# Two matmuls of 256 columns become one of 512 in the mixer, and the state-space scan runs in two blocks of 128 steps

## The chip, the cores and the metric

The kernel runs on one core of one Trainium2 chip. The metric is the device time of one execution in microseconds, the lower the better. A core has a matrix engine (TensorE, PE in the profile; its weight loads are shown apart as PEld), a vector engine (VectorE, DVE), an activation engine (ScalarE, ACT), a general engine (GpSimd, POOL) and a queue that starts transfers (SyncE, SP). The engines run side by side. Each works through its own list of instructions in order, and an instruction at the head of a list that has to wait holds up all behind it.

## What is computed

One layer over 256 tokens of width 2048, all in float32. A mixer with two parallel branches comes first, then a mixture-of-experts FFN.

```
h = rms_norm(x);  proj = h @ w_in                    # 2048 -> 512 + 1536 + 1536 + 2*2048
u_s5, x_lru, y_lru = proj[:512], proj[512:2048], proj[2048:3584]
g_s5, g_lru = sigmoid(proj[3584:] + b_gate)          # two gates of 2048
out_s5  = s5_branch(u_s5)                            # complex diagonal state space, 32 groups x 64 states
out_lru = rglru_branch(x_lru, y_lru)                 # conv of 4, two gates, real linear recurrence, * gelu(y_lru)
x = x + (g_s5 * (out_s5 @ w_proj_s5) + g_lru * (out_lru @ w_proj_lru)) @ w_out
x = x + moe(rms_norm(x));  return rms_norm(x)
# s5_branch: states_t = lam_bar * states_(t-1) + b_bar u_t;  y = real(c states) + d u;  gelu, then a GLU
```

## The kernel before

Tokens lie along the free dimension (256 columns, `T`), features along the 128 partitions, so an activation matrix of 2048 features is 16 tiles (`KD`) of 128 x 256. Matmuls use a rounded float32 type. To keep full precision each operand is held as a high part and a low part, and one product is three matmuls into the same bank (`mm3`, L103 to L106): high weight by high input, high weight by low input, low weight by high input. Each has 256 columns and its own weight load. Here a "triple" means these three. `split` (L93) makes the two parts of a weight: ACT copies 1024 (or 768) columns to the rounded type (L99), DVE subtracts (L100); four buffers hold halves of units ahead of PE. Every weight unit of 1 MB is loaded on SP's queue (`load_unit`, L140).

The mixer runs in these stages:

- The first four units give `u` (L174), and about 30 us on the tables of the state-space branch are made on DVE: powers of a rotation, `loc_*` for steps 0 to 16 inside a block and `blk_*` for 16 blocks (`powers`, L360; `d_loc` and `d_blk`, L386).
- Twelve heads of the recurrent branch follow in four groups of three (L570). A head takes three `in_unit`s (L398) of 16 triples each: its y part (into `part` through Gelu, L579), its x part (`lru_head`, L520, with the conv reading the bank directly) and one gate unit (`gate_lru`, L565; ACT reads the bank). After the first and second group stands `s5_chunk(0)` and `s5_chunk(1)` (L409), after the fourth `s5_chunk(2)`; four more gate units; then `s5_chunk(3)`.
- The projection of the recurrent branch (L602): 16 units of 12 triples, each taken out of its bank by one DVE instruction (L611).
- 16 more gate units into `gs5` (L613), the GLU (L624, 16 triples of `mm3` with the state-space output), and the projection of the state-space branch (L651): 16 outputs of four triples, each taken out of its bank by DVE (L662), added on POOL (L663), and cut into high and low parts by ACT and DVE (L648, L649).
- `w_out` (L726), where the moving operand is 512 columns of weight, and the experts, whose 201 MB are streamed.

`s5_chunk(c)` handles four slices of 128 states. For each slice PE projects `u` into a bank of PSUM (`mid`, L422); six DVE instructions of 256 elements rotate it (L430 to L435). Per pair of slices come two scans (real and imaginary, L444), a scan over the 16 block ends with 18 small instructions around it (L453 to L477), the two scans again, and six instructions of 512 to rotate back (L483 to L488). PE then multiplies by `c` (L493) and DVE adds the skip term (L495).

There are four `acc` banks, two `mid` and two `aux` banks of PSUM. The order of each engine's list isn't written by hand. A planner puts the instructions out in time order, ready ones first by priority, which is the order of the program, except where `tc.high_priority(AHEAD)` moves a block ahead (the splits, the loads, what empties an `in_unit`'s bank). Lines L611 and L662 and all of `s5_chunk` have no such mark. A tile with a `tag` takes one of `bufs` buffers; where none is free, the first write waits until the last reader of an earlier tile of that tag has run.

Of the kernel before, what the change touches and what calls it, by code (L numbers as in the profile page):

```python
# [9 lines left out]
F32 = mybir.dt.float32  # L10
# [8 lines left out]
P = 128  # L19
# [16 lines left out]
def block_kernel(  # L36
# [70 lines left out]

    def mm3w(ps, ahi, alo, whi, wlo, first, last):
        PE.matmul(ps, ahi, whi, start=first, stop=False)
        PE.matmul(ps, alo, whi, start=False, stop=False)  # L110
        PE.matmul(ps, ahi, wlo, start=False, stop=last)
# [22 lines left out]
    hT = [hp.tile([P, KD, T], F32R, name=f"hT_{w}") for w in ("hi", "lo")]  # L134
    hT_hi, hT_lo = ([t[:, k, :] for k in range(KD)] for t in hT)
# [169 lines left out]
    blk_c = tb_.tile([P, 16, LOC], F32, name="blk_c")  # L305
    blk_s = tb_.tile([P, 16, LOC], F32, name="blk_s")
# [53 lines left out]
    def powers(tc_, ts_):  # L360
# [3 lines left out]
        while n < 16:  # L364
# [13 lines left out]
    powers(loc_c, loc_s)  # L378
    V.tensor_copy(blk_c[:, :, 1], loc_c[:, :, 16])
    V.tensor_copy(blk_s[:, :, 1], loc_s[:, :, 16])  # L380
    powers(blk_c, blk_s)
    rho16 = t16("rho16")
    V.tensor_tensor(rho16, rho, rho, op=ALU.mult)
    for _ in range(3):
        V.tensor_tensor(rho16, rho16, rho16, op=ALU.mult)
    d_loc = tb_.tile([P, 16, 16], F32, name="d_loc")  # L386
    d_blk = tb_.tile([P, 16, 16], F32, name="d_blk")
    V.tensor_copy(d_loc, rho[:, :, None].to_broadcast([P, 16, 16]))
    V.tensor_copy(d_blk, rho16[:, :, None].to_broadcast([P, 16, 16]))
    V.memset(d_loc[:, :, 0], 0.0)  # L390
    V.memset(d_blk[:, :, 0], 0.0)
# [6 lines left out]
    def in_unit(u, a_hi=hT_hi, a_lo=hT_lo, bank=acc_bank):  # L398
        raw = load_unit(w_in[u], 2048)
        ps = bank()[:, :T]  # L400
        for hf in range(2):
            hi, lo = split(raw[:, hf * 1024:(hf + 1) * 1024], 1024)
            for kk in range(8):
                k = hf * 8 + kk
                cs_ = slice(kk * P, (kk + 1) * P)
                mm3(ps, hi[:, cs_], lo[:, cs_], a_hi[k], a_lo[k], k == 0, k == KD - 1)
        return ps

    def s5_chunk(c):  # L409
        yps[c] = aux_bank()  # L410
        SB = 2
        for sb in range(4 // SB):
            bz = mp.tile([P, 2, SB, T], F32, tag="bz", bufs=2, name=nm("bz"))
            gz = mp.tile([P, 2, SB, T], F32, tag="gz", bufs=2, name=nm("gz"))
            s0 = 4 * c + sb * SB
            for i in range(SB):
                s = s0 + i
                q = s % 4
                rows = slice(32 * q, 32 * q + 32)
                ps = mid_bank()  # L420
                for ri in range(2):
                    PE.matmul(ps[:, ri * T:(ri + 1) * T], bt[rows, c, ri, :], uT[rows, c, :], start=True, stop=True,  # L422
                              tile_position=(32 * q, 0))
                p3 = ps.rearrange("p (r j t) -> p r j t", r=2, t=16)
                lc = loc_c[:, s, None, 0:16].to_broadcast([P, 16, 16])
                ls = loc_s[:, s, None, 0:16].to_broadcast([P, 16, 16])
                tt = mp.tile([P, 2, T], F32, tag="st", bufs=2, name=nm("st"))
                ttv = tt.rearrange("p r (j t) -> p r j t", t=16)
                bzv = bz[:, :, i, :].rearrange("p r (j t) -> p r j t", t=16)
                V.tensor_tensor(ttv[:, 0], p3[:, 1], ls, op=ALU.mult)  # L430
                V.tensor_tensor(ttv[:, 1], p3[:, 0], ls, op=ALU.mult)
                V.tensor_tensor(bzv[:, 0], p3[:, 0], lc, op=ALU.mult)
                V.tensor_tensor(bzv[:, 1], p3[:, 1], lc, op=ALU.mult)
                V.tensor_tensor(bz[:, 0, i, :], bz[:, 0, i, :], tt[:, 0], op=ALU.add)
                V.tensor_tensor(bz[:, 1, i, :], bz[:, 1, i, :], tt[:, 1], op=ALU.subtract)  # L435
            d3 = mp.tile([P, SB * T], F32, tag="d3", bufs=1, name=nm("d3"))
            A.activation(d3.rearrange("p (s j t) -> p s j t", s=SB, t=16),
                         d_loc[:, s0:s0 + SB, None, :].to_broadcast([P, SB, 16, 16]), AF.Copy)
            bz4 = bz.rearrange("p r s (j t) -> p r s j t", t=16)
            gz4 = gz.rearrange("p r s (j t) -> p r s j t", t=16)  # L440

            def scan():
                for ri in range(2):
                    V.tensor_tensor_scan(gz[:, ri].rearrange("p s t -> p (s t)"), d3,  # L444
                                         bz[:, ri].rearrange("p s t -> p (s t)"), 0.0, op0=ALU.mult, op1=ALU.add)

            scan()

            w = lambda: mp.tile([P, SB, 16], F32, tag="cw", bufs=8, name=nm("cw"))
            bc, bs = blk_c[:, s0:s0 + SB, 0:16], blk_s[:, s0:s0 + SB, 0:16]  # L450
            gr, gi = gz4[:, 0, :, :, 15], gz4[:, 1, :, :, 15]
            t1, t2, yr, yi, vr, vi = w(), w(), w(), w(), w(), w()
            V.tensor_tensor(yr, gr, bc, op=ALU.mult)  # L453
            V.tensor_tensor(t1, gi, bs, op=ALU.mult)
            V.tensor_tensor(yi, gi, bc, op=ALU.mult)
            V.tensor_tensor(t2, gr, bs, op=ALU.mult)
            V.tensor_tensor(yr, yr, t1, op=ALU.add)
            V.tensor_tensor(yi, yi, t2, op=ALU.subtract)
            fl = lambda t: t.rearrange("p s j -> p (s j)")
            db = fl(d_blk[:, s0:s0 + SB, :])  # L460
            V.tensor_tensor_scan(fl(vr), db, fl(yr), 0.0, op0=ALU.mult, op1=ALU.add)
            V.tensor_tensor_scan(fl(vi), db, fl(yi), 0.0, op0=ALU.mult, op1=ALU.add)
            bc, bs = blk_c[:, s0:s0 + SB, 1:16], blk_s[:, s0:s0 + SB, 1:16]
            v_r, v_i = vr[:, :, 0:15], vi[:, :, 0:15]
            t1, t2, yr, yi = w(), w(), w(), w()
            t1, t2, yr, yi = t1[:, :, 0:15], t2[:, :, 0:15], yr[:, :, 0:15], yi[:, :, 0:15]
            V.tensor_tensor(yr, v_r, bc, op=ALU.mult)
            V.tensor_tensor(t1, v_i, bs, op=ALU.mult)
            V.tensor_tensor(yi, v_i, bc, op=ALU.mult)
            V.tensor_tensor(t2, v_r, bs, op=ALU.mult)  # L470
            V.tensor_tensor(yr, yr, t1, op=ALU.subtract)
            V.tensor_tensor(yi, yi, t2, op=ALU.add)
            rb = rho[:, s0:s0 + SB, None].to_broadcast([P, SB, 15])
            V.tensor_tensor(yr, yr, rb, op=ALU.mult)
            V.tensor_tensor(yi, yi, rb, op=ALU.mult)
            V.tensor_tensor(bz4[:, 0, :, 1:16, 0], bz4[:, 0, :, 1:16, 0], yr, op=ALU.add)
            V.tensor_tensor(bz4[:, 1, :, 1:16, 0], bz4[:, 1, :, 1:16, 0], yi, op=ALU.add)  # L477
            scan()
            lc = loc_c[:, s0:s0 + SB, None, 0:16].to_broadcast([P, SB, 16, 16])
            ls = loc_s[:, s0:s0 + SB, None, 0:16].to_broadcast([P, SB, 16, 16])  # L480
            tr = mp.tile([P, SB, T], F32, tag="st", bufs=2, name=nm("so"))
            ti = mp.tile([P, SB, T], F32, tag="st", bufs=2, name=nm("so"))
            V.tensor_tensor(tr.rearrange("p s (j t) -> p s j t", t=16), gz4[:, 1], ls, op=ALU.mult)  # L483
            V.tensor_tensor(ti.rearrange("p s (j t) -> p s j t", t=16), gz4[:, 0], ls, op=ALU.mult)
            V.tensor_tensor(bz4[:, 0], gz4[:, 0], lc, op=ALU.mult)
            V.tensor_tensor(bz4[:, 1], gz4[:, 1], lc, op=ALU.mult)
            V.tensor_tensor(bz[:, 0], bz[:, 0], tr, op=ALU.subtract)
            V.tensor_tensor(bz[:, 1], bz[:, 1], ti, op=ALU.add)  # L488
            for i in range(SB):
                s = s0 + i  # L490
                q = s % 4
                for ri in range(2):
                    PE.matmul(yps[c][32 * q:32 * q + 32, :T], cp[:, s, ri, :], bz[:, ri, i, :],  # L493
                              start=(ri == 0), stop=(ri == 1), tile_position=(0, 32 * q))
        V.scalar_tensor_tensor(uT[:, c, :], uT[:, c, :], col(C_S5D, c), yps[c][:, :T], op0=ALU.mult, op1=ALU.add)  # L495
# [24 lines left out]
    def lru_head(h, ps_in, p_):  # L520
# [7 lines left out]
        with tc.high_priority(AHEAD):  # L528
            A.activation(xc, ps_in, AF.Identity, bias=col(C_CONVB, h), scale=col(C_CONVW, 36 + h))
# [35 lines left out]
    def gate_lru(d):  # L565
        ps = in_unit(44 + d)
        with tc.high_priority(AHEAD):
            A.activation(part[:, d, :], ps, AF.Tanh, bias=hcol(C_BGATE, 16 + d), scale=0.5)
# [557 lines left out]
```

## Time and profile before

| | us |
|---|---|
| median of 3 runs (lowest, highest) | 1090.77 (1089.81, 1092.85) |
| the profiled execution | 1093.92 |
| its span, first to last instruction | 1092.1 |
| PE, DVE, ACT, POOL busy in it | 994.2, 645.6, 379.1, 75.6 |

All times of rows are microseconds from the start of the span, unless marked ns. A matmul's row gives its start and how long it lies in the pipeline (0.28 for 256 columns); the next starts long before that, so PE's pace is read from start to start. The same holds for DVE in a smaller measure: an instruction's row is some 0.08 to 0.09 longer than the distance to the next one's start.

### The profile page before, as it was taken

The page shows a single profiled execution, that of the slowest core. Times are in us where ns is not written, and L with a number is a line of the kernel's source. Part 1 is how long each engine was busy: PE and PEld are TensorE (multiplying, and loading weights), DVE is VectorE, ACT ScalarE, POOL GpSimd, SP SyncE. Part 2 cuts the span into 40 slices and gives each one's busy share as a digit, 9 for nine tenths or more (in the row PEclk, how much of TensorE's full clock was granted, in tenths as well). Part 3 has the DMA queues.
Part 4 walks back from the last instruction along what each step waited for, and adds up shares of the span by engine and source line. Part 5 has one row for each costly group of instructions (what it writes and reads, how often), then busy time and mean ns, then how long its engine had stood idle before and what let it go on. Part 6 is the DMA issues. An engine that isn't in the chain of part 4 may idle for free. (4 is left out here: it accounts for less than half of the span.)

```text
span 1092.1 us, 18171 instructions
## 1 busy us (share of the span) xinstructions
PE 994.2 (91%) x7435; PEld 749.4 (69%) x7435; DVE 645.6 (59%) x1356; ACT 379.1 (35%) x591; POOL 75.6 (7%) x76
## 2 busy tenths in 40 slices
PE   5999999999999999999999999999988979797872
PEld 5999899998989999998889945445443424343220
DVE  7899999999999964458544433333333312232225
ACT  5568547577633354445434110111110101011102
POOL 4001201223200000006000000000000000000000
PEclk9999999999999999999999999989998989999897
DMA  7655444454244555554979699999999999999991
GB/s 274 212 171 201 155 158 151 157 178 165 97 147 158 184 190 191 193 182 166 392 290 373 247 393 419 375 419 420 419 419 420 419 420 418 420 420 419 420 383 80
DMA packets 45164, 308.93 MB, mean 283 GB/s; under 512 B 5040, under 2 KB 6736, under 8 KB 9744
## 3 DMA queue, kind: packets, MB, share of 16 engines
q1 hardware_dynamic: 44784, 306.84, 72.5%
q8 instruction: 60, 0.98, 0.4%
q0 software_dynamic: 288, 0.85, 0.4%
q14 instruction: 32, 0.26, 0.1%
HBM read 305.57 MB, written 2.10 MB: 282 GB/s over the span
## 5 line engine op out<-in xcount | busy, mean ns | idle before, releaser
L100 DVE TENSOR_TENSOR wlo<-raw,whi 128x1024 fp32r<-128x1024 f32 (+1 forms) x194 | 230.2, 1189 | 98.0 <-ACT whi L99 97.6
L99 ACT ACTIVATE whi<-raw 128x1024 fp32r<-128x1024 f32 (+1 forms) x194 | 197.5, 1022 | 226.8 <-PE acc L105 163.5
L106 PE MATMUL acc<-hT_hi,wlo 128*128 128x256 f32 x848 | 238.8, 282 | 0.0
L105 PE MATMUL acc<-hT_lo,whi 128*128 128x256 f32 x848 | 238.8, 282 | 0.0
L104 PE MATMUL acc<-hT_hi,whi 128*128 128x256 f32 x848 | 238.2, 282 | 0.0
L990 DVE TENSOR_TENSOR once<-acc,once 128x512 f32<-128x512 f32 x128 | 79.8, 685 | 141.0 <-PE acc L986 141.0
L105 PEld LDWEIGHTS acc<-hT_lo,whi 128*128 128x128 f32 x848 | 159.6, 188 | 2.6 <-issue 2.6
L106 PEld LDWEIGHTS acc<-hT_hi,wlo 128*128 128x128 f32 x848 | 159.5, 188 | 2.1 <-issue 2.1
L104 PEld LDWEIGHTS acc<-hT_hi,whi 128*128 128x128 f32 x848 | 159.2, 188 | 2.4 <-issue 2.4
L104 PE MATMUL acc<-br,whi 128*128 128x256 f32 x336 | 95.9, 291 | 8.1 <-ACT br L177 7.7
L105 PE MATMUL acc<-br,whi 128*128 128x256 f32 x336 | 96.8, 290 | 2.4 <-DVE br L178 2.2
L106 PE MATMUL acc<-br,wlo 128*128 128x256 f32 x336 | 96.0, 290 | 2.2 <-DVE wlo L100 2.2
L986 PE MATMUL acc<-ysb,sct 32*128 32x512 f32 x512 | 95.9, 682 | 1.5 <-DVE once L990 0.8
L942 PE MATMUL mid<-eraw,once 128*32 128x512 f32 x512 | 66.0, 632 | 23.8 <-DMA eraw<-in_w_exp_dram 23.8
L918 PEld LDWEIGHTS aux<-sel,x 128*128 128x128 f32 x512 | 61.0, 195 | 31.0 <-issue 20.8
L974 PE MATMUL mid<-eraw,act 128*32 128x512 f32 x504 | 67.8, 658 | 10.2 <-DVE act L955 8.2
L942 PE MATMUL mid<-eraw,xTe 128*32 128x512 f32 x488 | 61.1, 616 | 16.5 <-DMA eraw<-in_w_exp_dram 16.5
L104 PEld LDWEIGHTS acc<-br,whi 128*128 128x128 f32 x336 | 65.7, 198 | 10.0 <-ACT br L177 7.7
L945 ACT ACTIVATE gus<-mid 128x512 f32<-128x512 f32 x32 | 19.1, 597 | 153.6 <-PE mid L942 153.6
L918 PE MATMUL aux<-sel,x 128*128 128x128 f32 x512 | 67.5, 285 | 5.3 <-DVE sct L967 5.3
L105 PEld LDWEIGHTS acc<-br,whi 128*128 128x128 f32 x336 | 66.1, 197 | 4.4 <-DVE br L178 2.7
L106 PEld LDWEIGHTS acc<-br,wlo 128*128 128x128 f32 x336 | 65.8, 197 | 4.0 <-DVE wlo L100 2.4
(352 smaller groups left out, 1307.0 us busy)
## 6 DMA issues: line engine op xcount, KB each, us to landing
eraw<-in_w_exp_dram SPq DMA_DIRECT2D x188, 1024.0 KB, 19.9
raw<-in_w_in_dram SPq DMA_DIRECT2D x59, 1024.0 KB, 4.9
raw<-in_w_out_dram SPq DMA_DIRECT2D x16, 1024.0 KB, 6.3
raw<-in_w_plru_dram SPq DMA_DIRECT2D x16, 768.0 KB, 4.2
raw<-in_w_ps_dram SPq DMA_DIRECT2D x4, 1024.0 KB, 5.0
once<-in_w_exp_dram SPq DMA_DIRECT2D x4, 1024.0 KB, 9.1
xt<-in_xT_dram SPq DMA_DIRECT2D x4, 512.0 KB, 8.7
x<-in_x_dram SPq DMA_DIRECT2D x2, 1024.0 KB, 7.5
```

What stands on the lines that cost most here:

```text
L99: A.activation(hi[:, :n], src, AF.Copy)
L100: V.tensor_tensor(lo[:, :n], src, hi[:, :n].bitcast(F32), op=ALU.subtract)
L104: PE.matmul(ps, whi, ahi, start=first, stop=False)
L105: PE.matmul(ps, whi, alo, start=False, stop=False)
L106: PE.matmul(ps, wlo, ahi, start=False, stop=last)
L918: PE.matmul(pt[:, kk * P:(kk + 1) * P], x1[h][:, k * P:(k + 1) * P], sel[b][:, h].rearrange("p e s -> p (e s)"), start=h == 0, stop=h == 1)
L942: mm = PE.matmul(ps[S * q:S * q + S, :], xT[e // B][:, 4 * j + q, es_], raw[:, q * 512:(q + 1) * 512], start=j == 0, stop=j == 3, tile_pos ...
L945: A.activation(gus[e], ps, AF.Copy)
L974: PE.matmul(ps[S * nb:S * nb + S, :], act[e][:, S * f:S * f + S], raw[:, bank(nb)], start=f == 0, stop=f == 1, tile_position=(0, S * nb))
L986: PE.matmul(sc[nb], sct[e][rows, h, :], ysb[e][rows, :], start=e == ex[0], stop=e == ex[-1], tile_position=(S * nb, 0))
L990: V.tensor_tensor(yacc[h][:, bank(nb)], sc[nb], old[:, bank(nb)], op=ALU.add)
```

## The change

`mm2` takes the high and low part of an input side by side as one moving operand of 512 columns for the high weight, and adds low weight by high input to the left half of the bank. `both` sums the two halves on DVE when the bank is emptied. `mm2` replaces `mm3` in every `in_unit`, in the recurrent branch's projection and in the state-space branch's projection; the first four units, the small matmuls of the heads and the GLU keep `mm3`. `hT` becomes one tile so that its parts lie in one access pattern.

`s5_chunk` now rotates by one table of 128 steps (`fc`, `fs`, made per chunk from `loc_*` and eight blocks), handles all four slices in two blocks of 128 steps, scans each block once, and carries the end of the first block into the first step of the second. Its tiles have one buffer each. What `both` leaves in the recurrent branch's projection goes to a tile `pl` that takes the buffers `fc` and `fs` by turns; the GLU's and the state-space projection's `tg` use the same two buffers.

```diff
+    def mm2(ps, whi, wlo, a2, first, last):
+        PE.matmul(ps, whi, a2, start=first, stop=False)
+        PE.matmul(ps[:, :T], wlo, a2[:, 0, :], start=False, stop=last)
+    def both(dst, ps):
+        V.tensor_reduce(dst, ps.rearrange("p (w t) -> p t w", w=2), axis=AX.X, op=ALU.add)
...
-    hT = [hp.tile([P, KD, T], F32R, name=f"hT_{w}") for w in ("hi", "lo")]
+    hT = hp.tile([P, 2, KD, T], F32R, name="hT")
...
-    powers(blk_c, blk_s)
-    rho16 = t16("rho16")
...
+    powers(blk_c, blk_s, 8)
+    V.tensor_tensor(hop_c, rho, blk_c[:, :, 8], op=ALU.mult)
+    V.tensor_tensor(hop_s, rho, blk_s[:, :, 8], op=ALU.mult)
...
     def s5_chunk(c):
+        fc = mp.tile([P, SB, HT], F32, tag="fc", name=nm("fc"))      # SB = 4, HT = 128
+        fs = mp.tile([P, SB, HT], F32, tag="fs", name=nm("fs"))
...
+        V.tensor_tensor(f4(fc), lc, bc, op=ALU.mult)
+        V.tensor_tensor(tt, ls, bs, op=ALU.mult)
+        V.tensor_tensor(f4(fc), f4(fc), tt, op=ALU.subtract)
+        V.tensor_tensor(f4(fs), ls, bc, op=ALU.mult)
+        V.tensor_tensor(tt, lc, bs, op=ALU.mult)
+        V.tensor_tensor(f4(fs), f4(fs), tt, op=ALU.add)
...
+        for i0 in range(0, SB, 2):
+            tt = t4()
+            for i in (i0, i0 + 1):
...
+                V.tensor_tensor(tt[:, :, i - i0, :].rearrange("p r (j t) -> p r j t", t=HT), p3,
+                                fs[:, None, None, i, :].to_broadcast([P, 2, 2, HT]), op=ALU.mult)
+                V.tensor_tensor(bz[:, :, :, i, :].rearrange("p j r t -> p r j t"), p3,
+                                fc[:, None, None, i, :].to_broadcast([P, 2, 2, HT]), op=ALU.mult)
+            for ri in range(2):
+                o = bz[:, :, ri, i0:i0 + 2, :]
+                V.tensor_tensor(o, o, tt[:, 1 - ri].rearrange("p s (j t) -> p j s t", t=HT), op=ALU.subtract if ri else ALU.add)
+        for j in range(2):
+            for ri in range(2):
+                V.tensor_tensor_scan(f2(gz[:, j, ri]), f2(d3), f2(bz[:, j, ri]), 0.0, op0=ALU.mult, op1=ALU.add)
+            if j == 0:
...
+        for j in range(2):
+            tt = t4().rearrange("p r s t -> p (r s t)").rearrange("p (r s t) -> p r s t", r=2, s=SB)
+            V.tensor_tensor(tt, gz[:, j], fs[:, None].to_broadcast([P, 2, SB, HT]), op=ALU.mult)
+            V.tensor_tensor(bz[:, j], gz[:, j], fc[:, None].to_broadcast([P, 2, SB, HT]), op=ALU.mult)
+            for ri in range(2):
+                o = bz[:, j, ri]
+                V.tensor_tensor(o, o, tt[:, 1 - ri], op=ALU.add if ri else ALU.subtract)
...
     def lru_head(h, ps_in, p_):
...
+            xi = lt("xi")
+            both(xi, ps_in)
+            ps_in = xi
...
     def gate_lru(d):
...
-            A.activation(part[:, d, :], ps, AF.Tanh, bias=hcol(C_BGATE, 16 + d), scale=0.5)
+            both(part[:, d, :], ps)
+            A.activation(part[:, d, :], part[:, d, :], AF.Tanh, bias=hcol(C_BGATE, 16 + d), scale=0.5)
...
     for d in range(KD):
         raw = load_unit(w_plru[d], 1536)
...
-        V.scalar_tensor_tensor(part[:, d, :], part[:, d, :], 1.0, ps, op0=ALU.add, op1=ALU.mult)
+        pl = mp.tile([P, T], F32, tag=("fc", "fs")[d % 2], name=nm("pl"))
+        both(pl, ps)
+        V.scalar_tensor_tensor(part[:, d, :], part[:, d, :], 1.0, pl, op0=ALU.add, op1=ALU.mult)
...
-                    mm3(ps, hi[:, cs_], lo[:, cs_], br_hi[k], br_lo[k], k == 0, k == 3)
-                tg = mp.tile([P, T], F32, tag="st", bufs=2, name=nm("tg"))
-                V.scalar_tensor_tensor(tg, gs5[:, d, :], 1.0, ps, op0=ALU.add, op1=ALU.mult)
+                    mm2(ps, hi[:, cs_], lo[:, cs_], br2[k], k == 0, k == 3)
+                tg = mp.tile([P, T], F32, tag=("fc", "fs")[dd], name=nm("tg"))
+                both(tg, ps)
+                V.scalar_tensor_tensor(tg, gs5[:, d, :], 1.0, tg, op0=ALU.add, op1=ALU.mult)
```

The y parts of the heads and the `gs5` units get the same `both` ahead of their activation as `gate_lru`.

## Rows read from the trace of the kernel before

**Rows 1.** The page's chart of 40 slices, busy tenths of PE, DVE, DMA
```profile
PE   5999999999999999999999999999988979797872
...
DVE  7899999999999964458544433333333312232225
...
DMA  7655444454244555554979699999999999999991
```

**Rows 2.** Sums over stretches: PE, PEld, DVE, ACT, POOL busy (count), granted clock, DMA share, GB/s
```profile
30.00:303.40 273.40, 269.35 (x2171) 258.22 (x2170) 263.60 (x622) 175.46 (x266) 44.86 (x37) 1.00 0.49 167
303.40:391.10 87.70, 85.52 (x653) 79.03 (x652) 84.11 (x180) 32.38 (x39) 0.00 (x0) 0.98 0.49 159
30.00:391.10 361.10, 354.87 (x2822) 337.25 (x2821) 347.71 (x801) 207.84 (x305) 44.86 (x37) 1.00 0.49 165
...
510.00:520.00 10.00, 7.61 (x28) 6.06 (x27) 9.01 (x16) 6.19 (x12) 2.75 (x4) 0.83 0.76 234
```

**Rows 3.** PE in time order (start, duration, instruction), first and last of two unbroken runs
```profile
439.81 0.28 PE L104 MATMUL acc<-hT_hi,whi 128*128 128x256 f32 x1
...
443.97 0.28 PE L106 MATMUL acc<-hT_hi,wlo 128*128 128x256 f32 x1
...
528.02 0.39 PE L109 MATMUL acc<-whi,br 128*128 128x512 f32 x1
...
533.68 0.39 PE L110 MATMUL acc<-whi,br 128*128 128x512 f32 x1
```

**Rows 4.** PE in time order where the projections and gates change over
```profile
303.41 0.28 PE L104 MATMUL acc<-br,whi 128*128 128x256 f32 x1
...
386.85 0.28 PE L106 MATMUL acc<-br,wlo 128*128 128x256 f32 x1
...
480.05 0.28 PE L104 MATMUL acc<-y_hi,whi 128*128 128x256 f32 x1
```

**Rows 5.** DVE in time order inside the state-space chunks
```profile
302.34 0.20 DVE L477 TENSOR_TENSOR bz<-bz,cw 128x30 f32<-128x30 f32 x1
302.47 2.34 DVE L444 TENSOR_TENSOR_SCAN gz<-d,bz 128x512 f32<-128x512 f32 x2
304.73 0.93 DVE L100 TENSOR_TENSOR wlo<-raw,whi 128x768 fp32r<-128x768 f32 x1
...
307.38 0.69 DVE L486 TENSOR_TENSOR bz<-gz,loc_c 128x512 f32<-128x512 f32 x1
307.98 0.95 DVE L100 TENSOR_TENSOR wlo<-raw,whi 128x768 fp32r<-128x768 f32 x1
308.85 0.69 DVE L487 TENSOR_TENSOR bz<-bz,so 128x512 f32<-128x512 f32 x1
...
311.26 0.42 DVE L431 TENSOR_TENSOR st<-mid,loc_s 128x256 f32<-128x256 f32 x1
311.59 0.42 DVE L432 TENSOR_TENSOR bz<-mid,loc_c 128x256 f32<-128x256 f32 x1
...
390.47 0.69 DVE L488 TENSOR_TENSOR bz<-bz,so 128x512 f32<-128x512 f32 x1
391.08 2.36 DVE L100 TENSOR_TENSOR wlo<-raw,whi 128x1024 fp32r<-128x1024 f32 x2
```

**Rows 6.** One line's instructions: L611, ns shortest/median/longest, first and last start
```profile
L611 DVE SCALAR_TENSOR_TENSOR part<-part,acc x16: 397/422/433, 315.1 to 390.1; 128x256 f32<-128x256 f32 x16
```

**Rows 7.** PE in time order: six of the last chunk's sixteen L493
```profile
394.45 1.06 PE L493 MATMUL aux<-bz,cp 128*32 128x256 f32 x6
```

**Rows 8.** One line's instructions: a sum or minimum over an axis on DVE, the largest here
```profile
L798 DVE TENSOR_REDUCE xi<-xe x1: 220/220/220, 616.4 to 616.4; 128x8 f32<-128x64 f32 x1
```

**Rows 9.** The state-space projection: L662 on DVE, then PE at its end
```profile
L662 DVE SCALAR_TENSOR_TENSOR tg<-gs,acc x16: 405/408/422, 492.3 to 511.8; 128x256 f32<-128x256 f32 x16
...
510.04 0.28 PE L106 MATMUL acc<-br,wlo 128*128 128x256 f32 x1
512.71 0.80 PE L109 MATMUL acc<-whi,br 128*128 128x512 f32 x1 [2.39 <-ACT whi L99]
```

## What the change should do to the time, worked out before it was run

> **What bounds the kernel now.** I read the chart of slices first. PE shows nine tenths through the mixer (the first half) and DMA nine tenths through the experts (the second half), while DVE shows nine tenths from the second slice to the fourteenth [rows 1]. So the experts wait for their bytes, and whatever the mixer gains or loses moves them as a block: their buffers lie where the mixer's tiles lay. In the mixer two engines are nearly full at once. From 30 us to 391.1 us, where the last state-space chunk's last sum has run, DVE is busy 347.7 of 361.1 us, 263.6 of 273.4 before the recurrent projection begins and 84.1 of 87.7 after that [rows 2]. PE isn't held up much by it: the chunks are work that the planner pushes back behind what PE needs, so DVE carries a backlog, and PE reaches the projection at 303.41 with one chunk and a half still to do. The projection runs beside that backlog: L611 empties a bank 16 times between 315.1 and 390.1, slipped in between chunk instructions [rows 4 to 6]. That is the place to watch.
>
> **PE, per triple.** In an unbroken run 35 steps of 256 columns take 4.16 us, 118.9 ns each; 25 steps of 512 take 5.66 us, 226.4 each [rows 3]. A triple goes from 3 x 118.9 = 356.7 ns to 226.4 + 118.9 = 345.3, which saves 11.4. Bounds: nothing, if 512 columns out of two separate stretches cost two of 256; 17 ns, if the second matmul also ran at half the 512 price (113.2). I take 11.4, since the only changed matmul then has a row of its own length. The triples: 56 units x 16, 16 x 12 and 16 x 4 are 1152, together 13.1 us (0 to 19.7).
>
> The trace's distance of 118.9 [rows 3] is what makes this worth anything. The Trainium skill ("TensorE: Matmul & The Clock Gate", Back-to-back issue gap) gives a warm gap of columns / 2.4 GHz + 2.5 ns, 109 and 216 ns; by that a triple saves only 2.5 ns and 1152 save an estimated 2.9 us. The rows lie above both figures.
>
> **DVE: what `both` costs.** It reads 512 elements of a bank. No reduction of that size is in the trace; the largest has 64 elements and takes 220 ns [rows 8]. An elementwise instruction of 512 takes 307.98 - 307.38 = 0.60 from start to start, one of 256 takes 0.33 [rows 5]. Ends: 0.33 (priced by the 256 elements that it writes) and 1.20 (two passes). I take 0.60, as its input has the size of that row. Count: 40 up to the recurrent projection (12 y, 12 x, 16 gates), 24.0 us; then 16, 16 and 16.
>
> The nearest reduction above is too small to show a rate. The Trainium skill ("VectorE: DVE Perf Modes", The perf-mode tier table) has `tensor_reduce` at one element a cycle from PSUM and nothing faster; by it the price is 512 / 0.96 GHz = 0.53 and a fixed part, so an estimated sum would be the same.
>
> **DVE: the chunks.** Prices from start to start [rows 5]: 0.33 for 256, 0.60 for 512, a scan of 512 (304.73 - 302.47) / 2 = 1.13, a split of 768 0.87, of 1024 1.18, a small one between 0.13 and its row's 0.20 (0.15 taken). An elementwise of 1024 is priced as the split of 1024 (twice a 512 would be 1.20). Before, a chunk has 24 of 256 (7.9), 12 of 512 (7.2), 8 scans (9.0), 36 small ones (5.4) and L495 (0.4): 29.9. After: 18 of 512 for the tables, the rotation and its sums (10.8), 4 scans (4.5), 5 small (0.8), 4 of 1024 (4.7), 4 of 512 (2.4), L495 (0.4): 23.6. Four chunks save 25 us (22 to 32 with the ends of the small ones and of the 1024). The shorter tables save about 14 small instructions, 2 us. ACT's and POOL's part of a chunk (one copy, one memset) lie beside this; ACT is busy 207.8 of 361.1 [rows 2].
>
> **Where the new wait stands.** `pl` takes the buffers `fc` and `fs`, one each. Chunk 3 stands ahead of the projection in the program, so it has those buffers first, and its last products read them almost to its end. Before, L611 wrote to `part`, which nobody held. Now the first `both` of the projection must wait for chunk 3. PE can fill four `acc` banks, then its list stops, with all that stands behind: twelve units of this projection, the gates, the GLU. DVE meanwhile works off the chunks, and the four split buffers are full after two units ahead, so nothing of later stages is done in the meantime. So the order that overlapped DVE's backlog with PE's projection is lost, and DVE's sum of work sets the point.
>
> That point: of the 347.7 us of DVE work to 391.1 take off 25 and 2, add 24.0, take off what would now come after the point: splits of ten units (20 x 0.87 = 17.4), three splits of the next stage (3.5), 16 x 0.33 of L611 (5.3). That leaves 318.5. Idle time was 9.8 before 303.4, 3.6 after [rows 2]; I keep 10 (ends 0 and 13.4). Chunk 3 lets go at 30 + 328.5 = 358.5 (342 to 365).
>
> From there on PE is alone: 0.6 for the first `both`, sixteen L493 at 1.06 / 6 = 0.18 (2.8) [rows 7], a cold clock (after the stop at 510 us the granted clock's mean over 10 us is 0.83, so 3.4 us at the lower level, 1.2 instead of 2.4 GHz, and 1.7 lost [rows 2]), then 12 units x 12 x 0.3453 = 49.7. The projection ends at 413.3. Before it was 386.85 + 0.12 = 386.97 [rows 4]. That is +26.3.
>
> **The rest.** Gates of `gs5`: 480.05 - 386.97 = 93.1 before [rows 4]; after 256 x 0.3453 = 88.4, as chunk 3's L493 are already paid. -4.7. Their `both` lie under PE: DVE there needs 2 x 1.18 + 0.60 of 5.5 us; without that cover it would be 9.6. GLU: 0. State-space projection: DVE already has L662 from 492.3 to 511.8 with splits and L649 between, while PE ends at 510.04 [rows 9]; 16 x 0.60 = 9.6 more. PE's last output needs the bank of the twelfth, so part of it goes past PE into `w_out`, where DVE has room. Ends 0 and 9.6; I take 3.5, nearer to the first, since only the first twelve count. POOL and ACT behind L662 start later by the same.
>
> Sum: 26.3 - 4.7 + 3.5 = +25 us. On the profiled execution 1093.9 + 25 = 1119; on the median of the three runs, 3.2 lower, **1090.8 + 25 = 1116**. Lower end: no idle (-10), chunks at their cheapest (-7), 17 ns a triple over the 400 behind the point (-2.3), nothing at the last step (-3.5): 1093. Upper: idle 13.4 (+3.4), chunks at their dearest (+3), no saving per triple (+4.6), 9.6 at the last step (+6): 1133.
>
> **Rivals.**
> *PE sets the time (faster).* If the projection isn't held by `pl`, because a buffer is free when PE has filled its four banks, all 13.1 count, less 3.5 at the state-space projection: 1081 (1074 to 1087). Its place is the first `both` of L602's loop. The point from which it decides: PE would have four outputs ready at about 303.4 - 640 x 0.0114 + 16.6 = 313, so chunk 3 would have to let go 45 us before the sum above, or `pl` get its buffer between two chunks. For it: DVE falls in total over the chunks. Against: 24 us of `both` take that back.
> *The reduction is dear (slower still).* At 1.20 per `both` the point moves by 24 and the last step by about 6: 1146. For it: no row of this size. Against: 220 ns for 64 elements fits one pass.
> *The change doesn't do what it says on PE.* If 512 columns in two stretches take 2 x 118.9, the main case goes to 1121; that lies in its range.
> *Chunks cancel.* Half the stall (chunk work much smaller than priced) and the PE gain together would give no change, about 1091; it would take 25 us less on DVE.
>
> **How the numbers follow.** Main case 0.70, PE sets the time 0.17, dear reduction 0.09, cancelling 0.04. A measurement here tells about 0.3% (3.3 us) from no change. Faster 0.18, within 0.04, slower 0.78. The range of 8 in 10 takes the main case and the upper half of the faster one: 1082 to 1132; the main case alone is 1093 to 1133.
>
> **What would show it.** Right: matmuls from `hT` in pairs of 226 and 119 ns; `both` at about 0.6; PE with a gap of tens of us after four outputs of the recurrent projection, ended by DVE on `pl`; L422 and L493 of chunk 3 inside that gap; the clock down after it; `gs5` about 88 us long. Wrong: no such gap and L611's successor interleaved with chunk 3 (faster case), `both` near 1.2, or DVE with long idle stretches before 300 us, which would mean that its sum didn't set the point.

## The result, and the profile of the changed kernel

The changed kernel takes 1120.82 us (median of 4 runs, 1119.59 to 1125.26); the kernel before, on the same chip, 1091.81. The ratio is 1.0271, with a 95% interval from 1.024 to 1.0302: slower by 29 us. The profiled execution took 1121.94 us, its span 1120.2.

The chart of slices (as [rows 1]) shows where. PE has a dent in the twelfth and thirteenth slice, 28 us each, and DMA falls to nothing in the second of them:

```profile
PE   5999999998862999998899999998998787988772
...
DVE  7998999999899775557844443332343132322225
...
DMA  7656354455230465554597979999999999999991
```

The sums by stretch (columns as in [rows 2]) put the dent between 330 and 370 us. The fourth column of times is DVE: it works all the while. PE stands, the granted clock is at its lower level (0.50 is 1.2 GHz), and the transfers stop, since the buffers that they fill wait for PE:

```profile
330.00:340.00 10.00, 1.95 (x16) 1.00 (x16) 9.97 (x13) 0.63 (x1) 0.10 (x1) 0.62 0.48 158
340.00:350.00 10.00, 3.84 (x14) 2.16 (x8) 9.61 (x16) 0.00 (x0) 0.00 (x0) 0.50 0.00 0
350.00:360.00 10.00, 0.00 (x0) 0.00 (x0) 9.93 (x16) 0.00 (x0) 0.00 (x0) 0.50 0.00 0
360.00:370.00 10.00, 8.04 (x43) 6.38 (x44) 7.88 (x15) 2.87 (x3) 0.00 (x0) 0.68 0.00 0
...
30.00:361.10 331.10, 292.52 (x1659) 247.90 (x1657) 315.95 (x607) 183.19 (x274) 48.23 (x41) 0.93 0.45 152
```

PE's list in time order, with the wait ahead of an instruction in brackets, tells who holds it. The last matmul of the fourth output of the recurrent projection starts at 328.79. Then only the last two chunks' own matmuls run (L481, L447), until the wait on `pl` ends:

```profile
328.79 0.28 PE L111 MATMUL acc<-br,wlo 128*128 128x256 f32 x1
338.05 2.56 PE L481 MATMUL aux<-bz,cp 128*32 128x256 f32 x16 [8.98 <-DVE bz L478]
343.96 3.23 PE L447 MATMUL mid<-uT,bt 32*128 32x256 f32 x8 [3.35 <-DVE bz L452]
361.96 0.77 PE L110 MATMUL acc<-br,whi 128*128 128x512 f32 x1 [14.77 <-DVE pl L115]
```

DVE's list shows what `pl` waited for: the first `both` of the projection (L115) follows directly on the last instruction that reads the table `fc` (L475).

```profile
358.85 1.23 DVE L474 TENSOR_TENSOR st<-gz,fs 128x1024 f32<-128x1024 f32 x1
360.00 1.22 DVE L475 TENSOR_TENSOR bz<-gz,fc 128x1024 f32<-128x1024 f32 x1
361.13 0.68 DVE L115 TENSOR_REDUCE pl<-acc 128x256 f32<-128x512 f32 x1
```

Three of the six groups of L115, one for each destination (duration in ns shortest/median/longest, first and last start), answer to [rows 6] and [rows 8]:

```profile
L115 DVE TENSOR_REDUCE part<-acc x26: 658/678/692, 58.5 to 314.6; 128x256 f32<-128x512 f32 x26
L115 DVE TENSOR_REDUCE pl<-acc x16: 677/691/692, 361.1 to 415.5; 128x256 f32<-128x512 f32 x16
L115 DVE TENSOR_REDUCE tg<-acc x16: 676/678/692, 517.6 to 545.5; 128x256 f32<-128x512 f32 x16
```

And PE where the stages change over (as [rows 4] and the last of [rows 9]): the first gate matmul at 415.26, the GLU at 505.13, `w_out` at 540.69.

```profile
415.14 0.28 PE L111 MATMUL acc<-br,wlo 128*128 128x256 f32 x1
415.26 0.39 PE L110 MATMUL acc<-hT,whi 128*128 128x512 f32 x1
...
505.13 0.28 PE L104 MATMUL acc<-y,whi 128*128 128x256 f32 x1
...
540.69 0.50 PE L118 MATMUL acc<-whi,br 128*128 128x512 f32 x1 [1.41 <-ACT whi L99]
```

### The profile page after: what moved, and what is told of

It is laid out like the page before. It is cut to its first block, busy times and chain, and to the rows that moved or that the text cites. A ratio compares the mean times of both kernels' runs of the same rounds, so it can differ in the third digit from the quotient of the medians.

```text
span 1120.2 us, 15788 instructions
## 1 busy us (share of the span) xinstructions
PE 987.4 (88%) x6283; PEld 693.5 (62%) x6283; DVE 674.1 (60%) x1252; ACT 377.0 (34%) x585; POOL 78.2 (7%) x80
## 5 line engine op out<-in xcount | busy, mean ns | idle before, releaser
L110 PE MATMUL acc<-hT,whi 128*128 128x512 f32 x848 | 304.3, 399 | 0.6 <-DVE xi L115 0.6
L100 DVE TENSOR_TENSOR wlo<-raw,whi 128x1024 fp32r<-128x1024 f32 (+1 forms) x194 | 228.1, 1181 | 90.1 <-ACT whi L99 89.8
L111 PE MATMUL acc<-hT,wlo 128*128 128x256 f32 x848 | 241.6, 286 | 0.7 <-DVE wlo L100 0.7
L110 PEld LDWEIGHTS acc<-hT,whi 128*128 128x128 f32 x848 | 161.5, 191 | 38.8 <-issue 3.0
L111 PEld LDWEIGHTS acc<-hT,wlo 128*128 128x128 f32 x848 | 161.9, 191 | 3.5 <-issue 1.7
L110 PE MATMUL acc<-br,whi 128*128 128x512 f32 x272 | 98.2, 403 | 20.6 <-DVE pl L115 14.8
L915 PEld LDWEIGHTS aux<-sel,x 128*128 128x128 f32 x512 | 61.5, 196 | 30.3 <-issue 24.1
L111 PE MATMUL acc<-br,wlo 128*128 128x256 f32 x272 | 76.8, 284 | 0.0
L971 PE MATMUL mid<-eraw,act 128*32 128x512 f32 x504 | 66.2, 644 | 11.8 <-DVE act L952 10.4
L110 PEld LDWEIGHTS acc<-br,whi 128*128 128x128 f32 x272 | 51.8, 191 | 35.1 <-issue 20.4
L915 PE MATMUL aux<-sel,x 128*128 128x128 f32 x512 | 68.0, 286 | 4.0 <-DVE sct L964 4.0
L983 PEld LDWEIGHTS acc<-ysb,sct 32*128 32x128 f32 x512 | 39.2, 203 | 35.3 <-issue 25.8
L118 PE MATMUL acc<-whi,br 128*128 128x512 f32 (+1 forms) x160 | 56.4, 353 | 1.4 <-ACT whi L99 1.4
L120 PE MATMUL acc<-wlo,br 128*128 128x512 f32 (+1 forms) x160 | 54.9, 356 | 2.3 <-DVE wlo L100 2.3
```

The costliest lines, as they stand in the source:

```text
L100: V.tensor_tensor(lo[:, :n], src, hi[:, :n].bitcast(F32), op=ALU.subtract)
L110: PE.matmul(ps, whi, a2, start=first, stop=False)
L111: PE.matmul(ps[:, :T], wlo, a2[:, 0, :], start=False, stop=last)
L915: PE.matmul(pt[:, kk * P:(kk + 1) * P], x1[h][:, k * P:(k + 1) * P], sel[b][:, h].rearrange("p e s -> p (e s)"), start=h == 0, stop=h == 1)
L971: PE.matmul(ps[S * nb:S * nb + S, :], act[e][:, S * f:S * f + S], raw[:, bank(nb)], start=f == 0, stop=f == 1, tile_position=(0, S * nb))
L983: PE.matmul(sc[nb], sct[e][rows, h, :], ysb[e][rows, :], start=e == ex[0], stop=e == ex[-1], tile_position=(S * nb, 0))
```

## Experiments

The table below gives, for each profile, the start of PE's first matmul of a stage (for the projection's end, of its last one), in us from the start of the span. The names e1 to e11 are those of the experiments below.

| kernel | projection begins | ends | GLU | `w_out` | experts | end of span | median of runs |
|---|---|---|---|---|---|---|---|
| before | 303.4 | 386.9 | 480.0 | 512.7 | 624.2 | 1092.1 | 1091.81 |
| after | 306.5 | 415.1 | 505.1 | 540.7 | 654.6 | 1120.2 | 1120.82 |
| `pl` of its own (e1) | 304.4 | 381.6 | 473.3 | 508.9 | 622.6 | 1088.0 | 1092.09 |
| scan only (e2) | 303.1 | 378.6 | 469.8 | 502.7 | 614.3 | 1079.9 | 1082.56 |
| wide only (e3) | 321.9 | 401.8 | 495.4 | 530.7 | 644.6 | 1116.6 | 1122.25 |
| cheap sum (e4) | 299.1 | 409.1 | 499.1 | 534.5 | 648.4 | 1117.3 | 1119.72 |
| late wide (e5) | 302.8 | 374.3 | 465.3 | 498.1 | 610.0 | 1078.8 | 1089.57 |
| wait only (e6) | 302.9 | 397.3 | 488.6 | 521.5 | 631.9 | 1106.9 | 1108.80 |
| copy, own buffer (e9) | 305.9 | 381.3 | 472.6 | 505.4 | 616.9 | 1086.2 | 1082.98 |

The kernel before, run again beside them, took 1093.09 (e1 to e4), 1093.40 (e5, e6, e8) and 1092.54 (e9 to e11). The theory at the start was the prediction's: the wait of `pl` for the last chunk stops PE, and DVE's sum of work sets when it ends. Its rivals: the extra work on DVE delays the mixer with or without that wait, or the wide matmul itself is at fault.

### The buffer (e1)

```diff
-        pl = mp.tile([P, T], F32, tag=("fc", "fs")[d % 2], name=nm("pl"))
+        pl = gsp.tile([P, T], F32, tag="pl", bufs=2, name=nm("pl"))
```

> The changed kernel, with the summed output of the recurrent projection in two buffers of its own, in the pool that holds the gates, instead of the two table buffers of the state-space chunks. Buffer theory: PE's stop from 328.8 to 362.0 us goes, the projection runs beside chunk 3 as in the kernel before, and the time falls by about 27 us to 1090 to 1097. DVE-sum theory (DVE's work ahead of that point holds PE whatever buffer it is): chunk 3 still ends near 360 us, PE still stops, 1112 or more.

Measured: 1092.09 us, ratio to before 0.9992 (0.9979 to 1.0005). One line of the program gives back 29 us. The sums into `pl` now run beside the last chunk, whose skip term comes at 412.5 only, and no wait of PE is longer than 1.6 us between 300 and 390. The group and the waits of PE there (engine, instruction, whom it waited for: us in total, times, longest):

```profile
L115 DVE TENSOR_REDUCE pl<-acc x16: 659/675/678, 321.0 to 384.0; 128x256 f32<-128x512 f32 x16
```
```profile
PE acc L110 <- DVE part L115: 1.6, 1, 1.6
PE acc L111 <- DVE wlo L100: 1.2, 3, 0.5
```

### Each half of the change alone (e2, e3)

The scan only: all of the new `s5_chunk`, but three narrow matmuls and no `both` anywhere.

```diff
     def mm2(ps, whi, wlo, a2, first, last):
-        PE.matmul(ps, whi, a2, start=first, stop=False)
-        PE.matmul(ps[:, :T], wlo, a2[:, 0, :], start=False, stop=last)
+        mm3(ps[:, :T], whi, wlo, a2[:, 0, :], a2[:, 1, :], first, last)
...
-        pl = mp.tile([P, T], F32, tag=("fc", "fs")[d % 2], name=nm("pl"))
-        both(pl, ps)
-        V.scalar_tensor_tensor(part[:, d, :], part[:, d, :], 1.0, pl, op0=ALU.add, op1=ALU.mult)
+        V.scalar_tensor_tensor(part[:, d, :], part[:, d, :], 1.0, ps[:, :T], op0=ALU.add, op1=ALU.mult)
```

> Only the state-space part of the change: two blocks of 128 steps, but three matmuls of 256 columns and no sums on DVE. If DVE's backlog is off PE's path as long as nothing waits for its end, 25 us less of DVE work give only the few microseconds of PE's short stops before 320 us: 1085 to 1090. If the backlog itself cost time in the kernel before, some 10 us or more would come back: 1080 or less.

Measured: 1082.56 us, ratio 0.9902 (0.9883 to 0.9922): 10.5 us faster than before, a time between the two that were written down. It beats both kernels. The GLU begins 10.2 us earlier. Adding up PE's distances from start to start up to the GLU, 6.4 of them lie in the chunks' output matmuls (64 records: 12.7 us before, 6.3 now), 1.8 in PE's waits after 30 us, and the rest in all other matmuls and at the start. The output matmuls are no fewer; they stand differently. Before, a pair of slices was issued at a time, to two groups of 32 columns; now four slices follow each other, to four groups, and the records start 7 to 14 ns apart where the group changes. In time order, six records of the kernel before took 1.06 us [rows 7]; here fourteen take 1.08:

```profile
361.38 1.08 PE L480 MATMUL aux<-bz,cp 128*32 128x256 f32 x14
```

The wide matmul only: `mm2` and `both` with the old chunks and tables, `pl` in buffers of its own as in e1.

```diff
+    [s5_chunk, powers, d_loc, d_blk as in the kernel before]
-        pl = mp.tile([P, T], F32, tag=("fc", "fs")[d % 2], name=nm("pl"))
+        pl = gsp.tile([P, T], F32, tag="pl", bufs=2, name=nm("pl"))
```

> Only the matmul part: one of 512 columns and one of 256 with the sum on DVE, the state-space chunks of the kernel before, and two own buffers for the projection's sums. DVE's work from 30 us to the end of chunk 3 grows by about 24 us plus 16 sums. If that is off PE's path: 1085 to 1093. If DVE is now so late that heads and projection wait for it: 1100 to 1115.

Measured: 1122.25 us, ratio 1.0266 (1.0245 to 1.0286). The projection begins 18.5 us later than before, because PE waits in the heads, for the small operands that DVE and ACT make (L551, L550), for splits (L100) and for a sum (L115):

```profile
PE mid L105 <- DVE xl L551: 6.1, 3, 3.0
PE mid L104 <- ACT xh L550: 5.0, 3, 2.0
PE acc L111 <- DVE wlo L100: 3.7, 4, 2.2
PE acc L110 <- DVE xi L115: 1.8, 1, 1.8
```

So 24 us more on a DVE without room slow the mixer without any buffer wait. The time lies above the 1100 to 1115 that were expected for this case. With the new chunks, e1 against e3, the kernel is 30 us faster; in the profiles 22.0 of 28.6 us are won before the experts, the rest in their stage (see e5, e10, e11). The parts don't add up: the scan alone gives 10.5 us, the wide matmuls on top of it take 9.5 (e1 against e2), the shared buffer another 28.7 (after against e1).

### The price of the sum (e4)

```diff
     def both(dst, ps):
-        V.tensor_reduce(dst, ps.rearrange("p (w t) -> p t w", w=2), axis=AX.X, op=ALU.add)
+        V.tensor_copy(dst, ps[:, :T])
```

> The changed kernel, but each sum only copies the left half of the bank (the product of high weight and low input is left out of the result), so that it takes about 0.33 us instead of 0.60. If DVE's sum of work sets the point at which chunk 3 lets go of the buffers, that point moves from 361.1 us to about 350 (40 x 0.27 = 10.8) and the time falls by 11 to 14 us, to 1107 to 1110. If PE or the chunk's own chain sets it, it stays within 3 us.

Measured: 1119.72 us, ratio 1.0235 (1.0212 to 1.0258), and the expectation was missed. Up to the first write to `pl`, DVE is busy 306.67 us instead of 315.95: 9.3 less, about as priced. But that write starts at 355.6 instead of 361.1, only 5.5 us earlier. DVE's idle time before it grew from 15.2 to 18.9 us. Between 276 and 306 us it waits for ACT, longer than in the changed kernel (where these four rows are 0.7, 0.2, 1.4 and 0.7):

```profile
DVE wlo L100 <- ACT whi L99: 3.4, 3, 1.7
DVE ti L542 <- ACT ti L534: 1.6, 2, 1.2
DVE pb L547 <- ACT pb L579: 1.4, 1, 1.4
DVE a L540 <- ACT a L538: 0.6, 1, 0.6
```

So DVE's sum sets the point only in the main. It runs close enough to PE and ACT in the last heads that some 4 of 9 us saved came back as waiting. At the experts 6.2 us were left of it, at the end of the span 2.9: the experts' stage took 468.9 us instead of 465.6.

### The wait without the wide matmul (e6, e9)

Both start from the scan-only kernel. e6 copies the projection's result into the tables' buffers; e9 is the same with two buffers of its own.

```diff
+        pl = mp.tile([P, T], F32, tag=("fc", "fs")[d % 2], name=nm("pl"))      # e6
+        pl = gsp.tile([P, T], F32, tag="pl", bufs=2, name=nm("pl"))           # e9
+        V.tensor_copy(pl, ps[:, :T])
-        V.scalar_tensor_tensor(part[:, d, :], part[:, d, :], 1.0, ps[:, :T], op0=ALU.add, op1=ALU.mult)
+        V.scalar_tensor_tensor(part[:, d, :], part[:, d, :], 1.0, pl, op0=ALU.add, op1=ALU.mult)
```

> The scan-only kernel with nothing but the buffer wait added: three narrow matmuls everywhere, no reduction; the projection's result is copied (0.4 us) into the buffers of the last chunk's rotation tables before the multiply-add. Theory (the wait alone stops TensorE, however wide the matmul): chunk 2 lets go of the tables near 313 us, chunk 3 runs 24.4 us in one piece on the vector engine as in the changed kernel, plus splits, so TensorE stands from the fourth output (near 321) to 340, and the projection ends near 392 instead of 378.6: 1096 us, between 1090 and 1102. Rival 1 (the stop comes from the reductions' 24 us, not from the buffer): 1083. Rival 2 (the wait costs what it costs in the changed kernel, 28 us): 1110.

> The wait-only kernel (1108.8 us) with one thing changed: the projection's copy goes into two buffers of its own instead of the last chunk's rotation tables. Sixteen copies of 0.42 us stay on the vector engine. Theory (the stop came from the buffer, not from the copies): TensorE has no wait over 2 us in the projection, which ends near 379 instead of 397.3, and the time is that of the scan-only kernel, 1082.6 us, between 1080 and 1086. Rival (the copies hold the last chunk and with it the projection): 1095 or more.

Measured: 1108.80 us (ratio 1.0147, 1.0121 to 1.0173) with the shared buffer, 1082.98 (0.9916, 0.9891 to 0.994) without, which is the scan-only kernel's time. The waits of PE between 300 and 400 us in e6, of which e9 shows none:

```profile
PE acc L104 <- DVE pl L600: 16.2, 1, 16.2
PE mid L446 <- DVE bz L451: 0.5, 1, 0.5
```

The two kernels differ in that one line. This settles the cause: neither the wide matmul nor the reduction is needed for the stop, the buffer alone makes it. The first copy starts at 340.63, as expected (340). The projection took 94.4 us against 75.4 in e9, 19 us more. The expectation of 1096 was 13 too low all the same: the projection ended 5 us later than worked out, and the experts' stage lasted 475.0 us against 465.6 in the scan-only kernel, a thing that the next three runs follow. The time is out of the theory's range and only 1 us from rival 2, but not by that rival's reason: in the changed kernel the projection took 108.6 us against 77.2 in e1, a stop worth 31 us and not 19.

### The wide matmul where DVE has room (e5, e10, e11)

```diff
+    def mmw(ps, whi, wlo, a2, first, last):
+        PE.matmul(ps, whi, a2, start=first, stop=False)
+        PE.matmul(ps[:, :T], wlo, a2[:, 0, :], start=False, stop=last)
...
-                mm2(ps, hi[:, cs_], lo[:, cs_], br2[4 + k], k == 0, k == HEADS - 1)
+                mmw(ps, hi[:, cs_], lo[:, cs_], br2[4 + k], k == 0, k == HEADS - 1)
+        pl = gsp.tile([P, T], F32, tag="pl", bufs=2, name=nm("pl"))
+        both(pl, ps)
...
-        ps = in_unit(28 + d)
+        ps = in_unit(28 + d, mm=mmw)
+            both(gs5[:, d, :], ps)
```

> The scan-only kernel (1082.56 us) with the wide matmul and its reduction put back only where the vector engine has room: the recurrent projection (sums into two buffers of their own) and the state-space gates behind it. TensorE saves 192 triples at 10 ns and 256 at 5.7 ns, the two savings measured in the changed kernel: 3.4 us. Theory (a sum costs nothing where no wait ends on the vector engine): 1079.2 us, between 1077 and 1081. Rival (16 sums in the projection push the last chunk back and with it a wait): 1082 to 1086.

Measured: 1089.57 us, median of 12 runs from 1080.64 to 1092.36, ratio 0.9959 (0.9937 to 0.998). The mixer does what was expected: the experts begin at 610.0 instead of 614.3. The total doesn't follow (the profile is of the fastest of the 12 runs). To tell chance from cause, both kernels ran again side by side.

> The scan-only kernel once more, beside the kernel with the late wide matmuls on one chip, to tell the two apart: in the profiles the late wide matmuls bring the experts forward by 4.3 us (610.0 against 614.3), but the span by 1.1 us only, since in their seventh ten microseconds the experts' stage ran at a granted clock of 0.67 instead of 1.00 and its weight stream at 228 GB/s instead of 408. Theory (the end is the weight stream's, 420 GB/s whenever it isn't held; a low clock at that place makes a hole in it): 1082.6 us, between 1081 and 1086, and more uniform than the other kernel. Rival (it varies just as much, and its four runs so far were lucky): median 1086 to 1090.

> The kernel with the late wide matmuls once more, beside the scan-only kernel on one chip. Theory (as the row above): runs spread again from 1080 to 1092 us with a median near 1089, and slower than the scan-only kernel although its experts start 4 us earlier. Rival (the chip made the difference): 1079 to 1081, faster than the scan-only kernel by 2 us.

Measured: scan only 1082.61 us (6 runs, 1080.58 to 1083.12; ratio 0.9904, 0.9871 to 0.9936), late wide 1088.08 (11 runs, 1080.32 to 1091.35; ratio 0.9931, 0.9903 to 0.9959). The kernel whose experts start 4 us earlier ends later, as the theory had it for both times. The two profiles, some 50 to 70 us after the experts' first matmul, differ most in one place (columns as in [rows 2]; the last three are granted clock, DMA share, GB/s). Late wide (experts from 610.6):

```profile
664.00:668.00 4.00, 4.00 (x16) 1.70 (x12) 1.13 (x2) 0.60 (x1) 0.00 (x0) 0.94 1.00 408
668.00:672.00 4.00, 4.00 (x11) 1.71 (x10) 0.69 (x1) 0.00 (x0) 0.00 (x0) 0.50 1.02 422
672.00:676.00 4.00, 4.00 (x10) 2.19 (x9) 1.29 (x2) 0.00 (x0) 0.00 (x0) 0.50 0.63 260
676.00:680.00 4.00, 4.00 (x13) 2.44 (x12) 1.38 (x2) 0.00 (x0) 0.00 (x0) 0.50 0.00 0
680.00:684.00 4.00, 3.64 (x20) 1.11 (x23) 1.06 (x4) 0.22 (x1) 0.00 (x0) 0.50 0.00 0
```

Scan only (experts from 614.5):

```profile
664.00:668.00 4.00, 4.00 (x30) 1.00 (x22) 1.92 (x6) 0.42 (x1) 0.00 (x0) 1.00 1.01 418
668.00:672.00 4.00, 4.00 (x26) 2.24 (x25) 1.30 (x3) 0.18 (x1) 0.00 (x0) 1.00 1.00 416
672.00:676.00 4.00, 3.78 (x20) 2.17 (x18) 3.23 (x7) 0.22 (x1) 0.00 (x0) 1.00 1.02 424
676.00:680.00 4.00, 3.76 (x36) 1.20 (x40) 0.78 (x4) 0.60 (x1) 0.00 (x0) 1.00 0.97 358
```

In the first the granted clock falls to its lower level while PE is busy without a break, and some 7 us later the stream of expert weights stops for about 10 us. The wait of SP's queue, where those transfers are issued, names the release of a weight buffer by PE's down-projection of an expert (L969 in the one, L962 in the other). Over the same 45 us of the stage, from 44 us after the experts began, the longest single wait (the last number) is 18.5 us in the late wide kernel and 9.4 in the scan-only one. The totals say less, since a queue that waits while its earlier transfers still run loses nothing:

```profile
SPq L699 <- PE mid L969: 25.7, 4, 18.5
```
```profile
SPq L692 <- PE mid L962: 33.3, 8, 9.4
```

Elsewhere between 20 and 430 us after the experts' first matmul the stream moves 415 to 427 GB/s in every ten microseconds of every profile, so what it loses there it can't make up. Counting what is missing to 420 GB/s between 60 and 80 us, as time, gives 10.4 us in e11, 9.2 in e6, 4.6 in e5, 2.9 before, 0.7 after and 0.3 in e2. The experts' stage lasted 475.8, 475.0, 468.8, 467.9, 465.6 and 465.6 us: taken off, 464.2 to 465.8 in these six, and 464.5 to 466.8 in e1, e3, e4, e8 and e10. One profile doesn't fit: e9 misses 0.6 us there and lasted 469.3; its extra 3 us lie in the last 30 us, where the stream has nearly run dry in every profile.

The clock isn't the only difference between the two kernels. The planner also put PE's list for the experts in another order, though no edit touches that part. The down-projection that frees the buffers is the fifth after the experts began. In e10 it starts 61.7 us after the experts' first matmul, in e11 70.5. e4 has the order of e11 between the fourth and the fifth (48 gather matmuls, L915 in e4, instead of 32) and a granted clock of 1.00 in the whole stage up to there. There it starts at 64.8, and the stream has a hole all the same. The fifth down-projection in e10, e4 and e11, then four microseconds of the hole in e4:

```profile
676.24 1.92 PE L962 MATMUL mid<-eraw,act 128*32 128x512 f32 x16 [0.46 <-DVE act L943]
```
```profile
713.13 1.92 PE L971 MATMUL mid<-eraw,act 128*32 128x512 f32 x16 [0.47 <-DVE act L952]
```
```profile
681.08 3.64 PE L969 MATMUL mid<-eraw,act 128*32 128x512 f32 x16 [0.36 <-DVE act L950]
```
```profile
712.00:716.00 4.00, 3.38 (x31) 1.14 (x34) 1.24 (x5) 0.82 (x2) 0.00 (x0) 1.00 0.35 88
```

All twelve profiles fall in line by these two things:

| PE's order there | granted clock, 60 to 70 us after the experts' first matmul | missing, us |
|---|---|---|
| as e10 | 1.00 (after, e1, e2, e9, e10) | 0.3 to 0.7 |
| as e10 | 0.83 (e8, before) | 1.9, 2.9 |
| as e11 | 1.00 (e4) | 4.4 |
| as e11 | 0.67 (e5, e3) | 4.6, 5.2 |
| as e11 | 0.50 (e6, e11) | 9.2, 10.4 |

By this table an estimated 4 of the 9.8 us between e10 and e11 go with the order and 6 with the clock. e5 and e11 are one program, and their two profiles (4.6 and 10.4 us missing) differ in the clock. It isn't shown that the clock alone makes a hole: no run forced it, and none changed only the order. What makes it fall in some executions and not in others stays open. e6 and e9, one line apart, differ in that order too: of the 25.8 us between them 5.7 lie in the experts' stage.

### The layout (e8)

```diff
-    hT = hp.tile([P, 2, KD, T], F32R, name="hT")
+    hT = hp.tile([P, KD, 2, T], F32R, name="hT")
...
-    y2 = mp.tile([P, 2, 4, T], F32R, tag="bz", name="y2")
+    y_hi = mp.tile([P, 4, T], F32R, tag="bz", name="y_hi")
+    y_lo = mp.tile([P, 4, T], F32R, tag="gz", name="y_lo")
```

> The changed kernel with buffers of its own for the projection's sum, and two layouts changed: the two halves of each input slice of the mixer lie beside each other (512 columns in one piece instead of two pieces 16 KB apart), and the gated linear unit's input is two tiles again. Theory A (the strided input costs TensorE the 4 to 6 ns a triple that were missing): state-space gates at 226 + 119 = 345 ns a triple instead of 230.6 + 120.6, their stage 88.4 us instead of 89.9; gated linear unit's matmuls 113 ns instead of 120. Theory B (the layout is nothing to TensorE): 230.6 + 120.6 and 89.9 us as before, 120 ns.

Measured in a single run: 1091.75 us, beside e1's 1092.09. The gates' matmuls stand 230.4 and 120.7 ns apart (means of 114 each), in e1 230.6 and 120.6; the projection's last start to the GLU's first is 91.7 us in both; the GLU's are at 120 ns still. Theory B holds: two separate stretches of 256 columns cost PE nothing that shows here.

## Why the prediction was right, and where not

Forecast: +25 us (1116.0 on the median). Measured: +29.0 on the medians, +28.1 on the spans, and in the profiles +28.3 at the end of the projection (forecast +26.3), -3.2 in the gates (-4.7), +0.6 in the GLU (0), +4.7 in the state-space projection and `w_out` (+3.5) and -2.3 in the experts (0). By the steps of the prediction:

- *The new wait.* Right, in its place, its cause and its form: four outputs, then nothing but chunk matmuls, ended by DVE on `pl`. e1 shows it by one line, e6 and e9 without the wide matmul.
- *When chunk 3 lets go.* Forecast 358.5, measured 361.1. DVE's busy time until then was 315.95, forecast 318.5; idle time was 15.2, where I kept 10. The idle term was the mis-sized one, and lay even above its upper end of 13.4: DVE waited for ACT's half of a split for 7.1 us in it (11 times), where the kernel before has 4.3 (7 times) up to its projection. With less on DVE still, in e4, the idle time grew again. That the point was missed by 2.6 us only is in part luck: a busy time 2.6 too high and an idle time 5.2 too low.
- *From there to the end of the projection.* Forecast 54.8 us, measured 415.26 - 361.13 = 54.1. The clock was down after the stop (0.68 in the ten microseconds of the restart).
- *PE per triple.* Forecast 345.3 ns. The rows of the gates, a pair of matmuls at a time:

```profile
437.01 0.39 PE L110 MATMUL acc<-hT,whi 128*128 128x512 f32 x1
437.24 0.28 PE L111 MATMUL acc<-hT,wlo 128*128 128x256 f32 x1
437.36 0.40 PE L110 MATMUL acc<-hT,whi 128*128 128x512 f32 x1
```

  The means over 114 pairs are 230.6 and 120.6 ns, together 351.2, so a triple saves 5.5 ns there instead of 11.4 (within the bounds of 0 to 17); in the projection 346.7, 10 ns saved. The row of 226.4 [rows 3] has `whi,br` with the weights as moving operand; e8 excludes the two stretches as the reason of the difference, and no run shows another.

  The Trainium skill ("TensorE: Matmul & The Clock Gate", Back-to-back issue gap) gives columns / 2.4 GHz + 2.5 ns for an isolated matmul, 216 and 109 ns. The rows lie 11 to 15 ns above that here, and the saving between the skill's 2.5 ns and the 11.4 of the rows before.
- *`both`.* 0.68 us by its row, 0.60 from start to start: as forecast, and the rival of the dear reduction is out.
- *The gates.* Forecast 88.4 us, measured 505.13 - 415.26 = 89.9; the difference is the triple's.
- *GLU.* Forecast 0, measured 6.03 us instead of 5.47. Its matmuls start 120 ns apart (median), before 113; they do so in e2 and e8 too, and the cause is open.
- *State-space projection and `w_out`.* Forecast +3.5. The stage itself took 29.5 instead of 27.2 us, +2.3, and `w_out` then lost 2.4 more, most of it in one wait for a split that stood behind the sums on DVE: +4.7, within its ends of 0 and 9.6.

```profile
544.17 0.80 PE L120 MATMUL acc<-wlo,br 128*128 128x512 f32 x1 [2.28 <-DVE wlo L100]
```

- *"The experts move as a block."* This step failed, though by little here: they began 30.4 us later and ended 28.1 later, as the hole in the weight stream was 2.9 us before and 0.7 after. For other kernels of this series it failed by more: the experts of e11 began 3.9 us ahead of e10's and ended 5.3 us behind them.
- *The rival "PE sets the time", 1081 us.* Its condition was made by e1, and gave 1092. The rival had left out that the heads wait longer for a full DVE: PE stands 7.0 us once, up to 280 us, for ACT's copy `xh`, which had itself waited for DVE's conv. It also counted 11.4 ns on all triples. What brings 1082.6 is the scan without the wide matmul. PE's longest wait in the heads of e1:

```profile
PE mid L104 <- ACT xh L526: 7.0, 1, 7.0
```

In the terms of the change: the halves of it pull against each other. The scan takes 27 us off DVE (busy 645.6 us before, 618.3 in e2; forecast 25 and 2) and halves the output matmuls' time on PE; the wide matmuls put 24 back on DVE, in the stretch where it has no room, and pay PE 6 to 10 ns a triple for it.

## What to carry to other kernels

A temporary that borrows a buffer must be read as a dependency: ask who has the buffer before it in program order, when that tile's last reader runs, and what stands in line behind the first write. Work moved from an engine with a steady stream to one that is nearly full pays only in stretches where the second has room, which is read from the sums by stretch and not from the share of the span. And where the end of a kernel is a saturated stream, a saving ahead of it counts only if the stream itself isn't interrupted: look for the slices in which its rate falls, and compare there the order of the instructions that free its buffers, which the planner can change far away from an edit.

## What the runs showed of the hardware

- Output matmuls to four groups of 32 columns, issued one after the other, start 7 to 14 ns apart where the group changes, and 64 of them took 6.3 us of PE's time instead of 12.7 when issued two groups at a time. It was worth more than the shorter waits.
- The stream of expert weights runs at 415 to 427 GB/s. The Trainium skill ("DMA: Bandwidth & Descriptors", Where 436 GB/s comes from) gives 435 GB/s as the ports' ceiling of a core; the trace lies 2 to 5% below it.
- The granted clock fell to 0.50 for at least 16 us in the experts of e11 with PE busy, by its records, 4.00 of 4.00 us in each of the four stretches up to 680; the same four stretches of e10 stayed at 1.00.
